# The low part of the down weights by an accumulating DMA from GpSimd

## Chip, cores and metric

The kernel runs on one core of a Trainium2 chip. The metric is the device time of one execution in microseconds; the table below has the median of three runs.

## What is computed

A decoder trunk of two layers over 512 tokens of width 1024: layer 0 mixes tokens by a gated delta rule, layer 1 by sliding-window attention, and both also attend to a memory. Each layer ends with a squared-ReLU MLP of hidden width 4096, and the down projection of that MLP is where the change lies:

```python
def sq_relu_mlp(h, w_up, w_down):
    return jnp.square(jax.nn.relu(h @ w_up)) @ w_down

...
        h = layer_norm(DN_ALPHA * h + sq_relu_mlp(h, mlp_w_up[layer], mlp_w_down[layer]),
                       ln_g[layer, 1], ln_b[layer, 1])
```

All of it is float32.

## The kernel before

TensorE multiplies in the format float32r, which keeps fewer bits than float32. So each operand is split into a high part (the value rounded to float32r) and a low part (the value minus the high part), and each product is made of three matmuls: high by high, high by low, low by high. For weights, `wload` (L81 to L89) makes the split: SyncE loads a slab of 128 x 1024 numbers (512 KB) into a buffer `wr`, ScalarE copies it into `wh` (L87, the rounding), and VectorE subtracts `wh` from `wr` into `wl` (L88). In the MLP the pool has four `wr` buffers and five each of `wh` and `wl`; each is used again as soon as its last reader is through.

`mlp` (L775 on) runs once per layer. The 4096 hidden features go in eight chunks c of 512. A chunk's down projection has two halves n of 512 output columns; each takes two slabs (`dn_slabs`, L947), and for each of four groups t of 128 tokens `down` (L936) makes 12 matmuls (`token_major`, L106 to L115: L112 reads `wh`, L113 `wl`, L114 `wh` with the low part of the hidden values) and VectorE adds the result to `res` (L945). Here one n of one c is called a half-chunk.

Between the down products stand the up products of the next chunk. They go by pairs of feature blocks in the class `Pair`: seven products m1 to m7 of 12 matmuls each (L866 to L868) into three PSUM tiles `upa`, `upb` and `upd`, on sums of weight blocks that GpSimd makes (`sa`, `sb`, L857 to L860) and that ScalarE and VectorE split at L118 and L119. In a steady half-chunk TensorE has m1, m6, m2, m5 and m7, then down for t = 0, m4, t = 1, m3, t = 2, t = 3. ScalarE copies the product m1 out of PSUM (L899) and VectorE adds it to `upb` (L905). The loop over c and n starts at L972; the first half-chunk of a layer has plain up products in place of a pair (`ups_second`, L816), and the last chunk (`downs_last`, L950) has no up products and takes four slabs at once.

The order on each engine is set by a scheduler that takes the program's order and the dependences; an engine works through its own list in order, and a wait holds up everything behind it. A buffer's next user waits for its last reader: a new `wh` for the L114 that read the old one, a new `wr` for the last reader of the old.

Of the kernel before, what the change touches and what calls it, by code (L numbers as in the profile page):

```python
# [11 lines left out]
F32 = mybir.dt.float32  # L12
F32R = mybir.dt.float32r
I32 = mybir.dt.int32
AF = mybir.ActivationFunctionType
ALU = mybir.AluOpType
AX = mybir.AxisListType

P = 128
# [30 lines left out]
def trunk(ctx: ExitStack, tc: tile.TileContext, xT, xn, memT, wk, wq, wv, wqm, wz, wmk, wmv, wo0, wo1, up, dn,  # L50
          bw, ws, conv, alog, dtb, nw, sinks, lng, lnb, lngb, pos, invf, out):
    nc = tc.nc
    V, G, A, T, SY = nc.vector, nc.gpsimd, nc.scalar, nc.tensor, nc.sync
# [8 lines left out]
    def nm(s):  # L62
        uid[0] += 1
        return f"{s}_{uid[0]}"
# [10 lines left out]
    def fr(ap):  # L75
        return ap.bitcast(F32)


    wpool = [None, 3, 4]

    def wload(src, shape):  # L81
        wp = wpool[0]
        raw = wp.tile(shape, F32, tag="wr", name=nm("wr"), bufs=wpool[1])
        SY.dma_start(raw, src)
        hi = wp.tile(shape, F32R, tag="wh", name=nm("wh"), bufs=wpool[2])
        lo = wp.tile(shape, F32R, tag="wl", name=nm("wl"), bufs=wpool[2])
        A.copy(hi, raw)  # L87
        V.tensor_sub(lo, raw, fr(hi))  # L88
        return hi, lo  # L89
# [685 lines left out]
    def mlp(pool, layer, last, gb0):  # L775
# [160 lines left out]
        def down(c, t, n, hid, slabs):  # L936
# [7 lines left out]
            else:  # L944
                V.tensor_tensor(dst, dst, ps, op=ALU.add)  # L945

        def dn_slabs(c, n):  # L947
            return [wload(dn[layer, c, n, i], [P, 2, 512]) for i in range(2)]

        def downs_last(hid):  # L950
            c = NC - 1
            slabs = [dn_slabs(c, n) for n in range(2)]
            late_out = []
            for t in range(NT):
                for n in range(2):
                    down(c, t, n, hid, slabs[n])
                    while late_out:
                        ln_out(*late_out.pop())
                if last:
                    mu, rs = ln_stats(t)  # L960
                    nmu = lns.tile([P, 1], F32, tag="nmu", name=nm("nmu"))
                    V.tensor_scalar(nmu, mu, -1.0, None, op0=ALU.mult)
                    late_out.append((t, nmu, rs, gb1))
                else:
                    ln_full(t, gb1)
            while late_out:
                ln_out(*late_out.pop())
# [4 lines left out]
        for c in range(NC - 1):  # L972
            later = new_hid()
            for n in range(2):
# [3 lines left out]
                if first:  # L978
                    ups_second(later)
                    slabs = dn_slabs(c, n)  # L980
                else:
                    p.m1()
                    p.m6()
                    p.split2()
                    slabs = dn_slabs(c, n)
                    p.m2()
                    p.m5()
                    p.m7()
# [26 lines left out]
    with tc.tile_pool(name="mlp0", bufs=2) as mpl:  # L1015
        mlp(mpl, 0, False, gb0)
# [185 lines left out]
    with tc.tile_pool(name="mlp1", bufs=2) as mpl:  # L1202
        mlp(mpl, 1, True, gb0)
# [71 lines left out]
```

## Time and profile before

| | |
|---|---|
| median of three runs (lowest to highest) | 1188.91 us (1188.09 to 1189.69) |
| the profiled execution's own time | 1191.65 us |
| its span, from the first to the last instruction | 1189.9 us |
| busy: TensorE, VectorE, ScalarE, GpSimd | 97%, 73%, 48%, 19% of the span |
| low parts by VectorE at L88 (all weights) | 136 in 166.4 us, 1225 ns each |
| copies to the high part at L87 | 136 in 142.5 us, 1051 ns each |
| loads of down weights | 64 of 512 KB, median 4.6 us from issue to landing |
| moved over the span | 114.17 MB, 96 GB/s |

In rows of a timeline the columns are the start in us from the span's start, the duration in us, the engine, the line, the operation, output and inputs, and in brackets how long the engine was idle before and for whom it waited. PE is TensorE (its matmuls overlap: the next starts before the row of one is over), DVE VectorE, ACT ScalarE, POOL GpSimd and SP SyncE; SPq is SyncE's queue.

### The profile page before, as it was taken

The page shows a single profiled execution, that of the slowest core. Times are in us where ns is not written, and L with a number is a line of the kernel's source. Part 1 is how long each engine was busy: PE and PEld are TensorE (multiplying, and loading weights), DVE is VectorE, ACT ScalarE, POOL GpSimd, SP SyncE. Part 2 cuts the span into 40 slices and gives each one's busy share as a digit, 9 for nine tenths or more (in the row PEclk, how much of TensorE's full clock was granted, in tenths as well). Part 3 has the DMA queues.
Part 4 walks back from the last instruction along what each step waited for, and adds up shares of the span by engine and source line. Part 5 has one row for each costly group of instructions (what it writes and reads, how often), then busy time and mean ns, then how long its engine had stood idle before and what let it go on. Part 6 is the DMA issues. An engine that isn't in the chain of part 4 may idle for free.

```text
span 1189.9 us, 19072 instructions
## 1 busy us (share of the span) xinstructions
PE 1158.1 (97%) x7512; PEld 1025.7 (86%) x7512; DVE 866.3 (73%) x1621; ACT 566.3 (48%) x1024; POOL 229.0 (19%) x180
## 2 busy tenths in 40 slices
PE   9899999999999999999999999999999999999996
PEld 8877788879998898998988888788989998989985
DVE  5478889777798666666656968886986666666657
ACT  5345454655484443545443346662653534445341
POOL 0112111101014413232220100000042314232204
PEclk9899999999999999999999999999999999999998
DMA  7522141204324232232424231112333242323311
GB/s 255 176 72 78 60 132 39 67 19 139 130 82 139 79 121 93 90 123 71 141 73 124 72 120 41 38 35 71 107 112 119 74 139 72 128 86 101 112 36 71
DMA packets 41242, 114.17 MB, mean 96 GB/s; under 512 B 12160, under 2 KB 12544, under 8 KB 41152
## 3 DMA queue, kind: packets, MB, share of 16 engines
q1 hardware_dynamic: 40576, 112.04, 28.9%
q8 instruction: 59, 0.97, 0.3%
q10 hardware_dynamic: 576, 0.92, 0.2%
q14 instruction: 31, 0.25, 0.1%
HBM read 109.53 MB, written 3.41 MB: 95 GB/s over the span
## 4 chain that ended last, share of the span: by engine, by line
PE 81%; DVE 11%; ACT 3%; DMA 1%; POOL 1%; issue 1%; POOLq 0%; SPq 0%; ACTq 0%; DVEq 0%
PE dn L113 9%; PE dn L114 9%; PE dn L112 9%; PE upb L866 3%; PE upb L867 3%; PE upb L868 3%; PE wo L113 2%; PE wo L114 2%; PE wo L112 2%; PE upa L867 2%; PE upd L867 2%; PE upa L868 2%; PE upd L868 2%; PE upa L866 2%; PE upd L866 2%; PE up L103 2%
## 5 line engine op out<-in xcount | busy, mean ns | idle before, releaser
L114 PE MATMUL dn<-wh,hl 128*128 128x512 f32 x512 | 200.0, 391 | 0.0
L113 PE MATMUL dn<-wl,hh 128*128 128x512 f32 x512 | 200.0, 391 | 0.0
L112 PE MATMUL dn<-wh,hh 128*128 128x512 f32 x512 | 199.6, 390 | 0.0
L87 ACT CAST wh<-wr 128x1024 fp32r<-128x1024 f32 (+1 forms) x136 | 142.5, 1051 | 103.8 <-PE dn L114 24.8
L88 DVE TENSOR_TENSOR wl<-wr,wh 128x1024 fp32r<-128x1024 f32 (+1 forms) x136 | 166.4, 1225 | 34.1 <-ACT wh L87 31.7
L114 PEld LDWEIGHTS dn<-wh,hl 128*128 128x128 f32 x512 | 96.1, 188 | 20.3
L945 DVE TENSOR_TENSOR res<-res,dn 128x512 f32<-128x512 f32 x120 | 82.0, 683 | 40.7 <-PE dn L114 40.2
L112 PEld LDWEIGHTS dn<-wh,hh 128*128 128x128 f32 x512 | 96.4, 188 | 17.6
L113 PEld LDWEIGHTS dn<-wl,hh 128*128 128x128 f32 x512 | 96.1, 188 | 17.7
L857 POOL TENSOR_TENSOR sa<-wr 128x512 f32<-128x512 f32 x26 | 36.1, 1388 | 370.6 <-DMA wr<-in_up_dram 279.6
L651 POOL TENSOR_TENSOR rs<-rs,nhalf 128x1 f32<-128x1 f32 x16 | 13.3, 834 | 338.1 <-DVE rs L650 282.0
L119 DVE TENSOR_TENSOR wl<-wr,wh 128x1024 fp32r<-128x1024 f32 x26 | 34.1, 1310 | 43.5 <-ACT wh L118 43.5
L118 ACT CAST wh<-sa 128x1024 fp32r<-128x1024 f32 x26 | 27.3, 1050 | 76.6 <-PE upd L867 76.6
L867 PE MATMUL upa<-XL,wh 128*128 128x256 f32 x208 | 58.5, 281 | 0.0
L867 PE MATMUL upd<-XL,wh 128*128 128x256 f32 x208 | 58.5, 281 | 0.0
L868 PE MATMUL upa<-XH,wl 128*128 128x256 f32 x208 | 58.4, 281 | 0.0
L868 PE MATMUL upd<-XH,wl 128*128 128x256 f32 x208 | 58.3, 280 | 0.0
L866 PE MATMUL upa<-XH,wh 128*128 128x256 f32 x208 | 58.3, 280 | 0.0
L866 PE MATMUL upd<-XH,wh 128*128 128x256 f32 x208 | 58.2, 280 | 0.0
L866 PE MATMUL upb<-TH,wh 128*128 128x256 f32 x208 | 58.0, 279 | 0.0
L867 PE MATMUL upb<-TL,wh 128*128 128x256 f32 x208 | 57.8, 278 | 0.0
L868 PE MATMUL upb<-TH,wl 128*128 128x256 f32 x208 | 57.6, 277 | 0.0
(411 smaller groups left out, 3365.7 us busy)
## 6 DMA issues: line engine op xcount, KB each, us to landing
wr<-in_up_dram SPq DMA_DIRECT2D x64, 512.0 KB, 5.4
wr<-in_dn_dram SPq DMA_DIRECT2D x64, 512.0 KB, 4.6
wr<-in_wo_dram SPq DMA_DIRECT2D x16, 512.0 KB, 3.8
wr<-in_bw_dram SPq DMA_DIRECT2D x8, 512.0 KB, 4.3
wr<-in_wz_dram SPq DMA_DIRECT2D x6, 520.0 KB, 4.5
wr<-in_wk_dram SPq DMA_DIRECT2D x6, 512.0 KB, 3.7
wr<-in_wq_dram SPq DMA_DIRECT2D x6, 512.0 KB, 3.5
wr<-in_wv_dram SPq DMA_DIRECT2D x6, 512.0 KB, 3.7
```

Source lines behind the costliest of these rows:

```text
L87: A.copy(hi, raw)
L88: V.tensor_sub(lo, raw, fr(hi))
L112: T.matmul(ps, sh, hi[:, kk, :], start=(k == 0), stop=False)
L113: T.matmul(ps, sh, lo[:, kk, :], start=False, stop=False)
L114: T.matmul(ps, sl, hi[:, kk, :], start=False, stop=(k == nk - 1))
L118: A.copy(hi, src)
L119: V.tensor_sub(lo, src, fr(hi))
L857: G.tensor_tensor(sa[:, 0], raw[1][:, kA], raw[1][:, kB], op=ALU.add)
L866: T.matmul(ps, hi[:, k, :], mh[:, k, :], start=start and k == 0, stop=False, skip_group_check=True)
L867: T.matmul(ps, hi[:, k, :], ml[:, k, :], start=False, stop=False, skip_group_check=True)
L868: T.matmul(ps, lo[:, k, :], mh[:, k, :], start=False, stop=stop and k == 3, skip_group_check=True)
L945: V.tensor_tensor(dst, dst, ps, op=ALU.add)
```

## The change

Only the down weights are loaded in a new way; all other weights keep `wload`. The raw slab is still loaded by SyncE and rounded by ScalarE. Then ScalarE writes the negated high part into `wl`, and a DMA issued from GpSimd reads the weights from memory once more and adds them onto it, so that `wl` holds the weights minus the high part.

```diff
+        def dn_load(src, shape):
+            wp = wpool[0]
+            raw = wp.tile(shape, F32, tag="wr", name=nm("wr"), bufs=wpool[1])
+            hi = wp.tile(shape, F32R, tag="wh", name=nm("wh"), bufs=wpool[2])
+            lo = wp.tile(shape, F32R, tag="wl", name=nm("wl"), bufs=wpool[2])
+            SY.dma_start(raw, src)
+            A.copy(hi, raw)
+            A.activation(lo, fr(hi), AF.Copy, scale=-1.0)
+            G.dma_start(lo, src, accum_op=ALU.add)
+            return hi, lo
+
         def dn_slabs(c, n):
-            return [wload(dn[layer, c, n, i], [P, 2, 512]) for i in range(2)]
+            return [dn_load(dn[layer, c, n, i], [P, 2, 512]) for i in range(2)]
```

The new function stands at L947 to L956, and lines behind it have numbers that are 11 higher. Where the instructions stand on ScalarE at the start of a steady half-chunk of layer 1, before (numbers in names tell buffers apart; `r` and `hh` are the hidden values of the pair before):

```order
L118 CAST hh_9417<-r_9477 128x1024
L87 CAST wh_9651<-wr_9649 128x1024
L87 CAST wh_9657<-wr_9655 128x1024
L899 COPY m_1465_9628<-upa_9615 128x256
L118 CAST wh_9740<-wr_9703 128x1024
L910 ACTIVATE r_9673<-upa_9615 128x256
```

and with the change:

```order
L118 CAST hh_9453<-r_9515 128x1024
L953 CAST wh_9688<-wr_9687 128x1024
L954 ACTIVATE wl_9689<-wh_9688 128x1024
L953 CAST wh_9695<-wr_9694 128x1024
L899 COPY m_1465_9666<-upa_9653 128x256
L954 ACTIVATE wl_9696<-wh_9695 128x1024
L118 CAST wh_9780<-wr_9743 128x1024
L910 ACTIVATE r_9713<-upa_9653 128x256
```

The first negation stands between the two copies, the second behind the copy of m1's product, `m`. On GpSimd there was before only the next pair's sums behind those of the last (in_dn_dram, below, is the weights in memory):

```order
L858 TENSOR_TENSOR sb_9512<-sa_9511,wr_9507 128x512
L860 TENSOR_TENSOR sb_9512<-wr_9507,sb_9512 128x512
L857 TENSOR_TENSOR sa_9707<-wr_9704 128x512
L859 TENSOR_TENSOR sa_9707<-wr_9703,wr_9704 128x512
L858 TENSOR_TENSOR sb_9708<-sa_9707,wr_9703 128x512
```

and with the change:

```order
L858 TENSOR_TENSOR sb_9550<-sa_9549,wr_9545 128x512
L860 TENSOR_TENSOR sb_9550<-wr_9545,sb_9550 128x512
L955 DMA wl_9689<-in_dn_dram 128x1024
L955 DMA wl_9696<-in_dn_dram 128x1024
L857 TENSOR_TENSOR sa_9747<-wr_9744 128x512
L859 TENSOR_TENSOR sa_9747<-wr_9743,wr_9744 128x512
```

Both DMAs stand ahead of the next pair's sums. The last place is ScalarE at the last chunk of layer 1, where four slabs are made; before:

```order
L87 CAST wh_11767<-wr_11765 128x1024
L87 CAST wh_11773<-wr_11771 128x1024
L932 ACTIVATE r_11643<-r_11643 128x768
L794 ACTIVATE r_11643<-r_11643 128x1024
L118 CAST hh_11387<-r_11643 128x1024
L87 CAST wh_11779<-wr_11777 128x1024
```

and with the change:

```order
L954 ACTIVATE wl_11828<-wh_11827 128x1024
L953 CAST wh_11834<-wr_11833 128x1024
L932 ACTIVATE r_11703<-r_11703 128x768
L954 ACTIVATE wl_11835<-wh_11834 128x1024
L794 ACTIVATE r_11703<-r_11703 128x1024
L118 CAST hh_11443<-r_11703 128x1024
L953 CAST wh_11841<-wr_11840 128x1024
L954 ACTIVATE wl_11842<-wh_11841 128x1024
```

The third slab's negation moved in between L932 and L794, ahead of the copy of the last hidden values and of the fourth slab.

## The prediction

> **What bounds the kernel now.** I read the page first: the span, the busy shares and the chain that ended last.
>
> ```profile
> span 1189.9 us, 19072 instructions
> PE 1158.1 (97%) x7512; PEld 1025.7 (86%) x7512; DVE 866.3 (73%) x1621; ACT 566.3 (48%) x1024; POOL 229.0 (19%) x180
> PE 81%; DVE 11%; ACT 3%; DMA 1%; POOL 1%; issue 1%; POOLq 0%; SPq 0%; ACTq 0%; DVEq 0%
> ```
>
> TensorE is busy for 97% of the span, and the chain is mostly its own matmuls. A share is an average, so next comes the view of the span in stages: a stretch of layer 1's MLP, the stretch between the MLPs, and the end.
>
> ```profile
> core 0: us, PE busy (x) PEld busy (x) DVE busy (x) ACT busy (x) POOL busy (x), PEclk, DMA share, GB/s
> 640.00:860.00 220.00, 215.10 (x1363) 183.11 (x1362) 181.56 (x471) 108.12 (x272) 7.52 (x8) 1.00 0.22 72
> 900.00:950.00 50.00, 50.00 (x311) 44.97 (x310) 33.75 (x39) 24.31 (x29) 18.25 (x12) 1.00 0.27 85
> 1140.00:1190.00 50.00, 39.55 (x203) 33.53 (x201) 33.32 (x52) 12.71 (x16) 12.66 (x12) 0.93 0.17 58
> ```
>
> In the MLP, where the change is, TensorE has no idle time (50.00 of 50.00), while VectorE works 33.75 of 50. So VectorE's work there is off the path, and the question is only whether the new way of making the low part is ready in time. For that I followed one half-chunk (the work of one n of one c) on TensorE and on the engines that feed it. TensorE's timeline:
>
> ```profile
> 928.46 0.39 PE L114 MATMUL dn<-wh,hl 128*128 128x512 f32 x1
> 928.68 0.28 PE L866 MATMUL upa<-XH,wh 128*128 128x256 f32 x1
> ...
> 935.92 0.40 PE L113 MATMUL dn<-wl,hh 128*128 128x512 f32 x1
> ...
> 937.29 0.39 PE L113 MATMUL dn<-wl,hh 128*128 128x512 f32 x1
> ```
>
> The old half-chunk's down products end at 928.68, five up products follow, and the new low parts are first read at 935.92 (slab 1) and, by the third of the product's four L113, at 937.29 (slab 2). ScalarE and VectorE make the slabs in between:
>
> ```profile
> 927.52 1.06 ACT L87 CAST wh<-wr 128x1024 fp32r<-128x1024 f32 x1 [0.24 <-PE dn L114]
> 928.88 1.05 ACT L87 CAST wh<-wr 128x1024 fp32r<-128x1024 f32 x1 [0.30 <-PE dn L114]
> 930.31 0.37 ACT L899 COPY m<-upa 128x256 f32<-128x256 f32 x1 [0.37 <-PE upa L868]
> 932.97 1.05 ACT L118 CAST wh<-wr 128x1024 fp32r<-128x1024 f32 x1 [2.29 <-PE upa L867]
> ...
> 928.61 1.23 DVE L88 TENSOR_TENSOR wl<-wr,wh 128x1024 fp32r<-128x1024 f32 x1
> 930.35 1.22 DVE L88 TENSOR_TENSOR wl<-wr,wh 128x1024 fp32r<-128x1024 f32 x1
> 931.75 0.42 DVE L905 TENSOR_TENSOR u<-m,upb 128x256 f32<-128x256 f32 x1 [0.18 <-PE upb L868]
> ```
>
> Both copies wait for TensorE to release a buffer, so a slab can't be prepared sooner than this. Before, the low parts are ready at 929.84 and 931.57, some 6.1 and 5.7 us before they are read. That slack is what the change spends.
>
> **The change part by part.** *Removed:* 64 subtractions on VectorE. By these rows that is 64 x 1.22 = 78 us, all in stages in which TensorE is never idle: worth nothing on the path. *Added on ScalarE:* 64 negations. I price them by the copy of the same tile, 1.05: 67 us beside 566, off the path except by what they delay. In the new order ScalarE runs copy 1, negation 1, copy 2, the copy of m, negation 2. Copy 1 ends at 928.58, negation 1 at 929.63, copy 2 at 930.68, m at 931.05 and negation 2 at 932.10. The next copy (932.97) isn't touched. The copy of m comes 0.37 later, so L905 ends at about 932.54. The product behind it that adds to upb is the last of the five, 7.0 / 5 = 1.4 us before 935.69, at 934.3: covered by 1.7 us, and past that each us would cost one.
>
> *Moved:* a wr buffer is free after the copy and not after the subtraction, so SyncE's loads start about 1.2 us earlier.
>
> ```profile
> 929.86 2.06 SPq L84 DMA_DIRECT2D wr<-in_dn_dram  x2
> 932.01 3.65 SPq L855 DMA_DIRECT2D wr<-in_up_dram  x2
> ```
>
> TensorE waits for none of these loads, so that is worth nothing; but they run from 928.6 on, just beside the new transfers.
>
> *Added on GpSimd:* 64 accumulating DMAs, each waiting for its negation, with TensorE waiting for them. Queued behind them on GpSimd are the four additions that make sa and sb; in this half-chunk they lie far from it:
>
> ```profile
> 924.18 1.31 POOL L860 TENSOR_TENSOR sb<-wr,sb 128x512 f32<-128x512 f32 x1
> ...
> 941.14 1.32 POOL L857 TENSOR_TENSOR sa<-wr 128x512 f32<-128x512 f32 x1 [15.65 <-DMA wr<-in_up_dram]
> ```
>
> GpSimd is idle from 925.5 to 941.1 and can issue at once. So transfer 1 has 935.92 - 929.63 = 6.3 us and transfer 2 937.29 - 932.10 = 5.2 us. Its latency L, from the issue to TensorE's release, is the disputed price; the trace shows no accumulating DMA and none from GpSimd. The nearest rows are plain loads of the same 512 KB:
>
> ```profile
> q1 hardware_dynamic: 40576, 112.04, 28.9%
> wr<-in_up_dram SPq DMA_DIRECT2D x64, 512.0 KB, 5.4
> wr<-in_dn_dram SPq DMA_DIRECT2D x64, 512.0 KB, 4.6
> L84 SPq DMA_DIRECT2D wr<-in_dn_dram x64: 327/328/384, 308.1 to 1139.7; - x64
> DMA to landing us min/median/max: 3.4/4.7/9.5
> ```
>
> The base is 4.6 us. An accumulation has to read two operands where a load reads one; a load's packets hold the 16 engines for 0.289 x 1189.9 x 0.524 / 112.04 = 1.6 us, so the second operand adds an estimated 1.6. GpSimd's share of issuing lies between SyncE's 0.33 and one of GpSimd's own additions, 1.3: I take 0.8. That makes 7.0. Transfer 2 is issued 2.5 us after transfer 1, whose packets then hold the engines for 3.2, so it finds 0.7 of them in its way: 7.7. Bounds: 3.4 (the fastest plain load, nothing added) to 9.5 + 1.6 + 1.3 + 0.7 = 13.1. I take 7.7, as the medians are from the same neighbourhood of other loads.
>
> The Trainium skill ("DMA: Bandwidth & Descriptors", "Anatomy of one DMA — SWDGE (gpsimd) path") gives 2.0 us + bytes / 436e3 for a DMA from GpSimd, an estimated 3.2 us for this size. By that rule the steady half-chunks cost nothing and the sum below is 2 x 0.7 = 1.4 us and not 74. The trace disagrees so far: no plain load of this size lands in under 3.4 us and the median is 4.6, so I stay with the rows.
>
> The sum. In a steady half-chunk transfer 1 is 0.7 late and transfer 2 is 7.7 - 5.2 = 2.5 us late; both stall the same stream, so the larger counts. There are 26 of them (13 in each layer): 26 x 2.5 = 65 us. The first half-chunk of a layer has room:
>
> ```profile
> 351.56 1.05 ACT L87 CAST wh<-wr 128x1024 fp32r<-128x1024 f32 x1 [0.47 <-PE up L103]
> 365.81 0.39 PE L113 MATMUL dn<-wl,hh 128*128 128x512 f32 x1
> ```
>
> With the negation the second slab is at 353.7, 12 us before its reading: nothing, and it would cost from L = 12 on. The last chunk makes four slabs, and the fourth is late:
>
> ```profile
> 1152.26 1.05 ACT L87 CAST wh<-wr 128x1024 fp32r<-128x1024 f32 x1 [7.30 <-PE upd L867]
> 1153.21 0.84 ACT L932 ACTIVATE r<-r 128x768 f32<-128x768 f32 x1
> 1154.08 1.06 ACT L794 ACTIVATE r<-r 128x1024 f32<-128x1024 f32 x1
> 1155.18 1.05 ACT L118 CAST hh<-r 128x1024 fp32r<-128x1024 f32 x1
> 1156.47 1.06 ACT L87 CAST wh<-wr 128x1024 fp32r<-128x1024 f32 x1 [0.24 <-PE dn L114]
> ...
> 1161.93 0.39 PE L113 MATMUL dn<-wl,hh 128*128 128x512 f32 x1
> ```
>
> The third negation now stands between L932 and L794, so the fourth copy ends at about 1158.4, its negation at 1159.4, and 2.5 us are left until 1161.93, the third L113 of that chunk's second product. With no transfer beside it L is 7.0: 4.5 us, twice, 9 us. Together 65 + 9 = 74 us. The profiled execution took 1191.65 (span 1189.9 and 1.75 around it) and would become 1265.7; it is 2.7 above the median of 1188.91, so the forecast for the median is **1263 us**.
>
> **The rivals.** *Hidden transfer.* If L stays at or below 5.2, the steady half-chunks cost nothing and only the last chunk pays, 2 x (L - 2.5): 1.8 us at 3.4 and 4.2 at 4.6, so 1190.7 to 1193.1. For it speaks that a plain load's median is below 5.2; against it, that the up loads already land at 5.4 and that nothing is then added for the second operand and the issue. This is also the case that the rule above of the Trainium skill leads to.
>
> *Much longer transfer.* If accumulation moves far slower than a load, or the two transfers and the loads at 929 to 935 delay each other, L goes to the upper bound of 13.1: 26 x 7.9 + 2 x (12.4 - 2.5) = 225 us, 1414. For it speaks the 9.5 us maximum of a plain load under others; against it, a DMA share of only 0.27 in the stage.
>
> *Faster, by relief of VectorE between the layers.* TensorE is idle for 4.9 us of 640 to 860. If the subtractions of layer 0's last slabs are what holds up VectorE there, their absence returns up to those 4.9 us: 1184. It decides only if L is below 5 as well, because otherwise the stalls outweigh it. Against it: VectorE has one such subtraction left in that stretch, 1.2 us.
>
> **How the numbers follow.** Forecast (L from 5.5 to 10) 0.52, much longer 0.23, hidden 0.20, relief 0.05. About 2.4 us, 0.2%, is what a measurement of this kernel can tell from no change. Hidden transfers are within that only at L below 3.7, so 0.08 of them counts as the same and 0.12 as slower: faster 0.05, same 0.08, slower 0.87. The range goes from 1192 (the relief and the shortest of the hidden transfers left out) to 1350, where transfer 2 has L = 10.8: 26 x 5.6 + 2 x 7.6 = 161 us, with the upper part of the much longer case left out.
>
> **What would show it.** Right: TensorE waits at L113 for a DMA, about 28 times, some 2.5 us each and some 4.5 in the two last chunks, and MLP stages in which it is no longer busy all the time; transfers that land in 7 to 8 us; ScalarE about 67 us busier and VectorE 78 us less. The forecast is wrong if the transfers land within 5 us and L113 waits for nothing, or if the wait is at another place: at upb for L905, at GpSimd's additions behind the DMAs, or at a load.

## The result, and the profile after

The changed kernel takes 1366.95 us (median of four executions, 1356.97 to 1377.81); the kernel before took 1188.70 beside it. The ratio is 1.146 (95% interval 1.1435 to 1.1491): slower, as forecast, but by 178 us where 74 were forecast, and outside the range. One execution of the changed kernel, in which the chip was in a slower state, is left out of the ratio. All rows below are from the execution of 1356.97, 165.3 us above the profiled one of before; two others took some 10 us more, at a mean granted clock of 0.94 where this one has 0.947.

The page of the changed kernel, in the order of the rows shown of before (span, busy shares, DMA queues, chain, and then the group of the low parts' matmuls and the loads):

```profile
span 1355.3 us, 19201 instructions
PE 1219.7 (90%) x7512; PEld 1056.5 (78%) x7512; DVE 829.1 (61%) x1557; ACT 622.6 (46%) x1088; POOL 273.8 (20%) x244
q1 hardware_dynamic: 40576, 112.04, 24.7%
q0 software_dynamic: 9216, 33.56, 14.1%
PE 54%; DMA 21%; DVE 9%; issue 9%; ACT 4%; POOL 2%; POOLq 0%; DVEq 0%; SPq 0%; ACTq 0%
L113 PE MATMUL dn<-wl,hh 128*128 128x512 f32 x512 | 221.2, 432 | 103.3 <-DMA wl<-in_dn_dram 103.3
wr<-in_dn_dram SPq DMA_DIRECT2D x64, 512.0 KB, 4.7
wl<-in_dn_dram POOLq DMA_DIRECT2D x64, 512.0 KB, 9.1
```

DMA had 1% of the chain that ended last and now has 21%. TensorE has the same 7512 matmuls, but they keep it busy for 1219.7 us instead of 1158.1. The new transfers land in 9.1 us while the plain loads still need 4.7. Their packets hold the 16 engines for 0.141 x 1355.3 x 0.524 / 33.56 = 2.98 us each, those of a load for 0.247 x 1355.3 x 0.524 / 112.04 = 1.57.

TensorE's waits, longest sum first:

```profile
PE dn L113 <- DMA wl<-in_dn_dram: 103.3, 55, 3.9
```

103.3 us of waiting and 61.6 us of longer matmuls (1219.7 - 1158.1) make 164.9 of the 165.3. The waits stand at the place that the prediction named; the longer matmuls stand around and behind them, and the prediction had none. ScalarE, GpSimd and SyncE in one steady half-chunk of layer 1:

```profile
1052.52 1.06 ACT L953 CAST wh<-wr 128x1024 fp32r<-128x1024 f32 x1 [0.24 <-PE dn L114]
1053.60 2.36 SPq L952 DMA_DIRECT2D wr<-in_dn_dram  x2
1053.60 1.06 ACT L954 ACTIVATE wl<-wh 128x1024 fp32r<-128x1024 f32 x1
1054.57 1.03 ACT L953 CAST wh<-wr 128x1024 fp32r<-128x1024 f32 x1
1054.96 0.88 POOL L955 DMA_DIRECT2D wl<-in_dn_dram  x1 [19.08 <-ACT wl L954]
1055.51 0.36 ACT L899 COPY m<-upa 128x256 f32<-128x256 f32 x1
1055.77 1.06 ACT L954 ACTIVATE wl<-wh 128x1024 fp32r<-128x1024 f32 x1
1057.12 0.86 POOL L955 DMA_DIRECT2D wl<-in_dn_dram  x1 [1.28 <-ACT wl L954]
1057.69 1.63 POOL L857 TENSOR_TENSOR sa<-wr 128x512 f32<-128x512 f32 x1
...
1060.58 3.77 SPq L855 DMA_DIRECT2D wr<-in_up_dram  x2
```

ScalarE runs in the order and at the pace of the working, and GpSimd issues as soon as a negation is done. But from 1053.6 on two loads of down weights are issued as well, and from 1060.6 on two of up weights. TensorE in the same half-chunk:

```profile
1053.68 0.28 PE L866 MATMUL upa<-XH,wh 128*128 128x256 f32 x1
...
1063.89 0.79 PE L113 MATMUL dn<-wl,hh 128*128 128x512 f32 x1 [2.82 <-DMA wl<-in_dn_dram]
1064.48 0.63 PE L114 MATMUL dn<-wh,hl 128*128 128x512 f32 x1
1064.91 0.63 PE L112 MATMUL dn<-wh,hh 128*128 128x512 f32 x1
...
1067.03 0.50 PE L113 MATMUL dn<-wl,hh 128*128 128x512 f32 x1 [0.21 <-DMA wl<-in_dn_dram]
1067.37 0.40 PE L114 MATMUL dn<-wh,hl 128*128 128x512 f32 x1
```

Transfer 1 is released 8.9 us after its issue (1054.96 to 1063.89), transfer 2 after 9.9 (1057.12 to 1067.03). Transfer 2 comes 13.35 us after the start of the half-chunk at 1053.68; the same reading stood at 8.61 before (937.29 - 928.68). Between the two, matmuls follow each other by 0.43 us instead of 0.23. The view by windows of 2 us shows why, in its column of the granted clock (PEclk, 1.00 is full speed), and how busy the 16 DMA engines are (their share can pass 1.00, as a packet counts whole where it starts):

```profile
core 0: us, PE busy (x) PEld busy (x) DVE busy (x) ACT busy (x) POOL busy (x), PEclk, DMA share, GB/s
1060.00:1062.00 2.00, 1.08 (x9) 0.76 (x7) 2.00 (x1) 0.00 (x0) 1.92 (x3) 1.00 1.01 246
1062.00:1064.00 2.00, 0.10 (x1) 0.11 (x1) 1.62 (x3) 0.00 (x0) 1.99 (x1) 0.89 1.07 217
1064.00:1066.00 2.00, 2.00 (x5) 1.61 (x6) 0.89 (x1) 1.05 (x1) 0.00 (x0) 0.50 0.90 340
1066.00:1068.00 2.00, 1.79 (x6) 0.93 (x6) 0.33 (x1) 0.00 (x0) 0.00 (x0) 0.76 0.49 199
1068.00:1070.00 2.00, 2.00 (x17) 1.87 (x16) 0.75 (x2) 0.19 (x1) 0.00 (x0) 1.00 0.02 6
```

The DMA engines are fully busy until the low parts are there and idle right after: it is a queue that is worked off. The granted clock falls to 0.50 near the end of the wait of 2.82 us and stays there for 0.44 + 2.00 + 0.96 = 3.4 us (a window's 0.89 means that 0.44 of its 2 us were at 0.50). The Trainium skill ("TensorE: Matmul & The Clock Gate", "Part 1: The HAM clock gate (the "warmup" mystery)") has it that the clock is halved after an idle window of about 3.4 us and comes back after as long a busy one. The rows agree on the 0.50 and on the 3.4 us, but not on the idle time: here the clock fell some 2.5 us into the idle stretch, which was over after 2.82.

In this half-chunk the low clock is over when transfer 2 is released. In others it is not; in the one that starts at 506.74 the release comes 12.78 us later, at 519.52, and the clock is still low in the window behind it:

```profile
518.00:520.00 2.00, 0.91 (x2) 0.48 (x2) 1.23 (x1) 0.15 (x1) 0.00 (x0) 0.50 0.95 375
520.00:522.00 2.00, 2.00 (x6) 1.52 (x6) 0.00 (x0) 0.00 (x0) 0.00 (x0) 0.50 0.06 23
```

Of the 26 steady half-chunks 22 have such a stretch at 0.50, nine of 3.4 us, twelve of 6.8 and one of 10.2. Four have none, though TensorE waited 1.9 to 2.8 us for transfer 1 in them.

**What the time went into.** The two steady stretches (from the first to the last start that TensorE's timelines show, 24 half-chunks) took 499.5 us before and 645.3 after, 6.07 more per half-chunk. Transfer 2 is released on average 13.52 us after the start (12.51 to 14.77), 4.91 late. The other 1.16 is the low clock that lasts beyond that release: nothing in half-chunks like the first one above, up to 2.8 us in others. The rest of the 61.6 us of longer matmuls costs nothing: those matmuls run between the two releases, where TensorE would otherwise wait for transfer 2.

### The profile page after: what moved, and what is told of

The parts are those of the page before. It is cut to its first block, busy times and chain, and to the rows that moved or that the text cites. A ratio compares the mean times of both kernels' runs of the same rounds, so it can differ in the third digit from the quotient of the medians.

```text
span 1355.3 us, 19201 instructions
## 1 busy us (share of the span) xinstructions
PE 1219.7 (90%) x7512; PEld 1056.5 (78%) x7512; DVE 829.1 (61%) x1557; ACT 622.6 (46%) x1088; POOL 273.8 (20%) x244
## 3 DMA queue, kind: packets, MB, share of 16 engines
q1 hardware_dynamic: 40576, 112.04, 24.7%
q0 software_dynamic: 9216, 33.56, 14.1%
## 4 chain that ended last, share of the span: by engine, by line
PE 54%; DMA 21%; DVE 9%; issue 9%; ACT 4%; POOL 2%; POOLq 0%; DVEq 0%; SPq 0%; ACTq 0%
DMA wl<-in_dn_dram 20%; PE dn L113 7%; PE dn L114 6%; PE dn L112 6%; PE wo L113 2%; PE wo L114 2%; PE wo L112 2%; PE up L103 2%; PE up L104 2%; PE up L102 2%; DVE y L315 1%; POOL wl L955 1%; PE upb L866 1%; PE upb L867 1%; PE upb L868 1%
## 5 line engine op out<-in xcount | busy, mean ns | idle before, releaser
L113 PE MATMUL dn<-wl,hh 128*128 128x512 f32 x512 | 221.2, 432 | 103.3 <-DMA wl<-in_dn_dram 103.3
L113 PEld LDWEIGHTS dn<-wl,hh 128*128 128x128 f32 x512 | 102.8, 201 | 148.2 <-DMA wl<-in_dn_dram 130.1
L114 PE MATMUL dn<-wh,hl 128*128 128x512 f32 x512 | 214.5, 419 | 0.0
L955 POOL DMA_DIRECT2D wl<-in_dn_dram x64 | 56.0, 875 | 575.0 <-ACT wl L954 508.6
L119 DVE TENSOR_TENSOR wl<-wr,wh 128x1024 fp32r<-128x1024 f32 x26 | 97.3, 3744 | 46.0 <-ACT wh L118 46.0
L88 DVE TENSOR_TENSOR wl<-wr,wh 128x1024 fp32r<-128x1024 f32 (+1 forms) x72 | 87.6, 1221 | 26.8 <-ACT wh L87 26.3
L87 ACT CAST wh<-wr 128x1024 fp32r<-128x1024 f32 (+1 forms) x72 | 75.2, 1050 | 57.4 <-PE kq L103 13.9
L953 ACT CAST wh<-wr 128x1024 fp32r<-128x1024 f32 x64 | 66.8, 1044 | 41.4 <-PE upd L867 24.3
L118 ACT CAST wh<-sb 128x1024 fp32r<-128x1024 f32 x26 | 27.2, 1047 | 113.6 <-POOL sb L860 113.6
L118 ACT CAST w2h<-wr 128x512 fp32r<-128x512 f32 x26 | 16.1, 620 | 132.2 <-PE upb L867 132.2
L954 ACT ACTIVATE wl<-wh 128x1024 fp32r<-128x1024 f32 x64 | 67.7, 1058 | 0.9
L651 POOL TENSOR_TENSOR rs<-rs,nhalf 128x1 f32<-128x1 f32 x16 | 12.2, 764 | 254.1 <-DVE rs L650 241.8
```

Of the source, the lines that this page charges most:

```text
L113: T.matmul(ps, sh, lo[:, kk, :], start=False, stop=False)
L114: T.matmul(ps, sl, hi[:, kk, :], start=False, stop=(k == nk - 1))
L118: A.copy(hi, src)
L119: V.tensor_sub(lo, src, fr(hi))
L955: G.dma_start(lo, src, accum_op=ALU.add)
```

## The experiments

The theory: the transfers are late because they share the DMA engines with four loads, and TensorE's clock falls behind the waits. The rivals: accumulation is slow in itself; the traffic harms something other than L113; the landing only follows TensorE's pace. Each kernel is the changed one with the edit shown. Times are medians, ratios are against the kernel before on the same chip.

**e1_fill: work in place of the wait.** Fourteen repeats of the first matmul of each t = 0 product stand ahead of it.

```diff
+            if t == 0:
+                for _ in range(14):
+                    T.matmul(ps, hh[:, 0, sl], slabs[0][0][:, 0, :], start=True, stop=True)
```

> TensorE repeats the first matmul of each half-chunk's first down product 14 times ahead of it (3.2 us of extra work a half-chunk, the result unchanged), so that it is busy while it would wait. If the wait itself lowers the granted clock: the wait at L113 shrinks from 103 us to under 30, the clock stays at 1.0 in the MLP, the matmuls behind it keep their 0.23 us pitch, and the time falls by 40 to 70 us, to about 1300. If the clock falls for another reason (the traffic, the power): the clock of the stage stays near 0.93 and the time is 1357 or more.

Measured: 1302.58 us, ratio 1.0945 (1.0921 to 1.0969), 64 us faster than the changed kernel with 448 matmuls more. The group of the matmuls that read the low parts (busy time, mean ns, wait), before and then in e1_fill:

```profile
L113 PE MATMUL dn<-wl,hh 128*128 128x512 f32 x512 | 200.0, 391 | 0.0
L113 PE MATMUL dn<-wl,hh 128*128 128x512 f32 x512 | 201.4, 393 | 6.3 <-DMA wl<-in_dn_dram 6.3
```

The mean is 393 ns here, 391 before and 432 in the changed kernel; the granted clock over the span is 0.995, and 0.947 in the changed kernel. 448 repeats at 0.228 us are 102; with the 6.3 and the span of before, 1189.9, this gives 1298.2, and the span is 1298.3. So without idling there is no loss to the clock. The 64 us are more than the low clock's 1.16 per half-chunk, because the low parts also came sooner: slab 2 could be read 12.2 to 13.4 us after the start in the six of 13 half-chunks of layer 0 that waited, and by 11.9 in the others. Why sooner, no run shows.

**e2_no_raw: no loads of raw down slabs.** The high part is copied from numbers that lie on the chip already, and the accumulation makes the low part to fit, so the products keep their work.

```diff
...
-            SY.dma_start(raw, src)
-            A.copy(hi, raw)
+            A.copy(hi, fr(XH[:, 0:2, :]))
...
```

> The raw down slabs are not loaded (the high part is copied from another tile, so the down products are of other numbers); the negations and the accumulating DMAs stay. If the 9.1 us of a transfer come from sharing the DMA engines with the loads: it lands in 5.5 to 7 us and the time is 1200 to 1270. If accumulation itself is that slow: it still lands in 8.5 us or more and the time stays within 30 us of 1357.

Measured: 1253.38 us, ratio 1.0527 (1.0494 to 1.0560).

```profile
wl<-in_dn_dram POOLq DMA_DIRECT2D x64, 512.0 KB, 5.8
```

The landing falls from 9.1 to 5.8, and transfer 2 is released 9.76 us after the start (mean of ten half-chunks of layer 0) instead of 13.25 in the same layer. The two loads left out held the engines for 2 x 1.57 = 3.1 us; the release came 3.5 sooner.

**e3_plain: a plain copy from GpSimd.** Without `accum_op` the DMA overwrites the negated part; the subtraction is left out.

```diff
-            G.dma_start(lo, src, accum_op=ALU.add)
+            G.dma_start(lo, src)
```

> The same DMA from GpSimd without the accumulation: it overwrites the negated part with the weights, so the low part is not the low part. If the second operand costs only engine time: the packets of a transfer hold the engines for about 1.6 us in place of 3.0, it lands in 6.5 to 7.5 us and the time is 1240 to 1290. If the add is slow in itself: it lands in 5 us or less, as a load from SyncE does, and the time is below 1210.

Measured: 1257.50 us, ratio 1.0576 (1.0514 to 1.0637). The transfers land in 7.3 us, hold the engines for 1.65 us each and are issued in 0.55 us instead of 0.87. So the second operand is worth 1.3 us of engine time and 1.8 of landing, and a DMA from GpSimd beside the four loads is late even without it: TensorE still waits 46.8 us for these transfers.

**e6_one_slab and e7_halves: less, and the same in pieces.** In the first only the second slab of a pair goes the new way; in the second each accumulation is cut into two of 256 KB.

```diff
-            return [dn_load(dn[layer, c, n, i], [P, 2, 512]) for i in range(2)]
+            return [f(dn[layer, c, n, i], [P, 2, 512]) for i, f in enumerate((wload, dn_load))]
```

```diff
-            G.dma_start(lo, src, accum_op=ALU.add)
+            for k in range(2):
+                G.dma_start(lo[:, k], src[:, k], accum_op=ALU.add)
```

> Slab 1 of each half-chunk is made as before (VectorE), slab 2 with the accumulating DMA, the result unchanged. By late transfers plus lower clock: one transfer a half-chunk, with some 5.9 us until it is read and about 7.5 us to land beside the loads, so 1.6 us of waiting and 1 us of lower clock in 26 half-chunks and a few us more in the last chunks: 1240 to 1290. If a transfer's latency is not made longer by the others: it stays at 9 us and the time is above 1300.

> Each slab's accumulation is issued as two DMAs of 256 KB, the result unchanged. If the sharing of the engines sets the landing: the first half is there earlier, the four together end as late as the two did, and the time falls by 10 to 40 us, to about 1330. If a fixed cost for each transfer and GpSimd's issue set it: the last lands 1 to 2 us later than before and the time is 1360 to 1420.

Measured: 1242.90 us, ratio 1.0436 (1.0388 to 1.0483), and 1360.36 us, ratio 1.1404 (1.1357 to 1.1452). One slab lands in 7.5 us and is released 10.19 after the start (mean of ten). Halves gain nothing, where the sharing of the engines had been expected to let them gain 10 to 40 us: the first half could be read sooner, but the last is released 14.3 to 15.0 us after the start in 23 of the 26 half-chunks, and each costs GpSimd 1.05 us to issue. GpSimd's last issue ends 5.1 us after the start instead of 4.3, and the engine time of a half-chunk is 12.8 us instead of 12.2.

**e4_unread, e8_short_sums and e9_late_read: nobody waits at t = 0.** In e4_unread the down products read `wh` in place of `wl`. e8_short_sums adds to this that GpSimd's sums are cut to an eighth and the splits of `sa` and `sb` read XH instead. In e9_late_read only t = 0 reads `wh`. Each leaves out what it doesn't read: the low part of the down weights, in e9 for t = 0 alone, and in e8 the sums too. The edit of e9_late_read:

```diff
-            token_major(ps, slabs, lambda k: hh[:, k, sl], lambda k: hl[:, k, sl])
+            use = [(h, h) for h, _ in slabs] if t == 0 else slabs
+            token_major(ps, use, lambda k: hh[:, k, sl], lambda k: hl[:, k, sl])
```

> All transfers run, but the down products read the high part in place of the low part, so nobody waits for them. If the waits and the clock behind them are the whole loss: 1188 to 1196, with a granted clock of 0.99. If the traffic, the negations or GpSimd's work slow something else as well: above 1210.

> As the kernel in which nobody reads the accumulated low part, and besides GpSimd's four sums are cut from 128x512 to 128x64 numbers each, with the two splits of the sums reading another tile in their place (the up products are then of other numbers). If VectorE's subtraction of the raw up slab, 3.7 us there in place of 1.2, is slow because GpSimd's sums run beside it: it is back at 1.2 to 1.4 us, TensorE no longer waits for VectorE at the last upb product, and the time is 1188 to 1200. If the transfers or their issue slow it: it stays above 3 us and the time above 1240.

> The changed kernel, except that the down product of t = 0 reads wh in place of wl; t = 1 to 3 read wl as before, so the low part is first read some 4 us later and all DMAs, buffers and splits stay (left out: the low part of the down weights in the first quarter of the tokens). It replaces the run in which nobody read wl and VectorE got the buffer of an unread low part. Theory (the time is lost in waiting at L113 and in the low clock behind it, the transfers' traffic itself costs nothing else): budgets of 10.3 and 9.2 us against a median landing of 9.1, so most waits are gone: 1190 to 1215 us, granted clock 0.99, VectorE no longer waiting for the transfers. Rival (the traffic of the new transfers slows other things as well: loads, GpSimd's sums, VectorE): still over 1235 us, with TensorE waiting at upb or upa.

Measured: 1263.40 us, ratio 1.0603 (1.0568 to 1.0638); 1259.70, ratio 1.0582 (1.0554 to 1.0611); 1220.79, ratio 1.0248 (1.0202 to 1.0294). The first two missed what was expected of the theory, by 67 and 60 us. A group of e4_unread shows that the edit had made a new wait:

```profile
L119 DVE TENSOR_TENSOR wl<-wr,wh 128x1024 fp32r<-128x1024 f32 x26 | 35.1, 1352 | 167.8 <-DMA wl<-in_dn_dram 159.9
```

A low buffer that nobody reads is free when its transfer lands, VectorE's next low part took just this buffer, and TensorE waited for VectorE (51.8 us at `upb`). Short sums didn't change that (162.1 us of the same wait). So these two runs say nothing on the traffic. e9_late_read keeps a reader for each buffer, and there the waits stand where t = 1 reads slab 2. Two of them, on TensorE's timeline:

```profile
500.66 0.50 PE L113 MATMUL dn<-wl,hh 128*128 128x512 f32 x1 [0.52 <-DMA wl<-in_dn_dram]
522.51 0.50 PE L113 MATMUL dn<-wl,hh 128*128 128x512 f32 x1 [0.60 <-DMA wl<-in_dn_dram]
```

Transfer 2 is released 13.1 to 14.8 us after the start wherever there is a wait (eleven of the 13 half-chunks of layer 0). The landing is as late with TensorE running on as with TensorE waiting. Given 4.2 us more, the kernel is 146 us faster than the changed one, the clock is 0.989, and 21.5 us of waits are left. TensorE's next longest wait, 2.7 us at another place, is in the kernel before too, so the traffic harms little else. The time is 6 us above the expected range because 4.2 us don't quite cover the 4.9.

**e5_from_sbuf and e12_loads_held: the engines for the accumulations alone.** e5_from_sbuf adds the raw slab on the chip instead of reading memory again; `wr` is then held until the landing, and so SyncE's next loads wait. e12_loads_held reads memory as before, but holds `wr` in the same way, by a DMA of 512 bytes that overwrites one column of it behind the landing.

```diff
-            G.dma_start(lo, src, accum_op=ALU.add)
+            G.dma_start(lo, raw, accum_op=ALU.add)
```

```diff
             G.dma_start(lo, src, accum_op=ALU.add)
+            SY.dma_start(raw[:, 0, 0:1], fr(lo)[:, 0, 0:1])
```

> The accumulating DMA reads the weights from the raw slab on the chip and not from memory again, the result unchanged. The raw buffer is then held until the transfer has landed, so the next loads start behind it and not beside it. If the loads beside it make the transfer late: it lands in 5.5 to 7 us and the time is 1220 to 1290. If the second operand and the add make it late: it lands in 8.5 us or more and the time is 1340 or more. If the loads that start later become the wait: TensorE's feeders wait for wr and the time is above 1360.

> The changed kernel, the accumulation from memory as it is, but each raw slab is held until its transfer has landed: a DMA of SyncE then writes one column of wl over the first column of wr, which nobody reads any more, so that the next load into this buffer, and the up loads behind it on SyncE, start after the landing. Nothing is left out; 64 DMAs of 512 bytes are added. In the changed kernel six transfers of 512 KB share the 16 DMA engines from the start of a half-chunk: two loads of down weights and two of up weights at 1.57 us of engine time each, and two accumulations at 2.98, 12.2 us in all, and transfer 2 is released 13.3 us after the start. Theory (the landing is set by this queue of engine time): the two accumulations have the engines for themselves, 6.0 us, and land in about 5.5 us, 9 to 10 us after the start, as in e5_from_sbuf: 1225 to 1250 us. Rival (e5 gained by its source on the chip, not by its later loads; reading memory for an accumulation is slow in itself): landing 7.5 us or more and 1280 us or more.

Measured: 1231.02 us, ratio 1.0348 (1.0321 to 1.0375), and 1269.31 us, ratio 1.0675 (1.0647 to 1.0703). The landings, of e5_from_sbuf and then of e12_loads_held:

```profile
wl<-wr POOLq DMA_DIRECT2D x64, 512.0 KB, 5.4
```

```profile
wl<-in_dn_dram POOLq DMA_DIRECT2D x64, 512.0 KB, 6.0
```

The timeline of e12_loads_held in its first steady half-chunk, which starts at 375.01:

```profile
376.74 0.89 POOL L955 DMA_DIRECT2D wl<-in_dn_dram  x1 [17.52 <-PE upa L868]
378.91 0.86 POOL L955 DMA_DIRECT2D wl<-in_dn_dram  x1 [1.28 <-ACT wl L954]
...
382.06 0.47 SPq L956 DMA_DIRECT2D wr<-wl  x1
382.70 0.48 SPq L952 DMA_DIRECT2D wr<-in_dn_dram  x1
...
385.08 0.50 PE L113 MATMUL dn<-wl,hh 128*128 128x512 f32 x1 [1.30 <-DMA wl<-in_dn_dram]
```

The loads start at 382.7, behind transfer 1, and transfer 2 is released 10.07 us after the start (11.0 on average, as the negations come later in the other half-chunks). The same DMA from the same memory lands in 6.0 us instead of 9.1 when the loads stand behind it: this is the separation that was wanted, and the rival "slow in itself" falls. The Trainium skill ("DMA: Bandwidth & Descriptors", "Issuing engines are not separate DMA queues") says that DMAs of all issuing engines run on the same 16 DMA engines and interleave; these rows agree. The expected time was missed by 19 us: held loads make the up weights and ScalarE late in turn. ScalarE waits 147.7 us for up weights, and TensorE waits for ScalarE's copy of m, which it never did in the changed kernel:

```profile
PE dn L113 <- DMA wl<-in_dn_dram: 36.6, 33, 2.6
PE upa L866 <- ACT m L899: 16.6, 18, 1.8
```

**e11_lo_last and e10_sbuf_lo_last: the low parts read last.** In the t = 0 product the four matmuls with `wl` come after the eight with `wh`; e11 on the changed kernel, e10 on e5_from_sbuf.

```diff
...
+                ks = [(s, kk, 2 * s + kk) for s in range(len(slabs)) for kk in range(2)]
+                for s, kk, k in ks:
+                    T.matmul(ps, hh[:, k, sl], slabs[s][0][:, kk, :], start=(k == 0), stop=False)
+                    T.matmul(ps, hl[:, k, sl], slabs[s][0][:, kk, :], start=False, stop=False)
+                for s, kk, k in ks:
+                    T.matmul(ps, hh[:, k, sl], slabs[s][1][:, kk, :], start=False, stop=(k == ks[-1][2]))
...
```

> The changed kernel with the order of e10_sbuf_lo_last alone: the four matmuls with wl last in the product of t = 0, the accumulation from memory as it is; nothing is left out. Theory: in a steady half-chunk transfer 1 is 2.8 us late and transfer 2 hardly at all behind it; transfer 1 gains 1.6 us, transfer 2 0.7, so each stall is 0.7 to 1.6 us shorter, 20 to 40 us in all, and the clock falls less behind shorter waits, another 20 to 40 us of the 62: 1290 to 1325 us. Rival (as for e10): 1350 or more.

> The accumulation takes the raw slab on the chip as its source (as in e5_from_sbuf), and in the product of t = 0 the four matmuls with wl come after the eight with wh; nothing is left out. The low part of slab 1 is read 7 matmuls later (1.6 us), that of slab 2 3 matmuls later (0.7 us). Theory: e5 waited some 0.7 us per half-chunk for transfer 2 and that wait goes: 1231 becomes 1203 to 1215, clock 0.99 to 1.00; what is left are the last chunk of a layer, where a transfer was 5.1 us late, and the copy of m behind the negations. It isn't faster than the kernel before. Rival (the landing moves with TensorE's own pace, so that a later reading is met by a later landing): 1225 or more.

Measured: 1366.52 us, ratio 1.1474 (1.1445 to 1.1503), and 1236.47 us, ratio 1.0369 (1.0336 to 1.0402). Both missed: nothing was gained. By their times alone both would speak for the rival, that the landing follows TensorE's pace; their traces show other reasons. In e11 the waits moved (TensorE, in the half-chunk that starts at 1002.60):

```profile
1012.86 0.73 PE L946 MATMUL dn<-wl,hh 128*128 128x512 f32 x2 [1.26 <-DMA wl<-in_dn_dram]
1015.99 1.22 PE L946 MATMUL dn<-wl,hh 128*128 128x512 f32 x2 [2.40 <-DMA wl<-in_dn_dram]
1017.01 0.41 PE L866 MATMUL upb<-TH,w2h 128*128 128x256 f32 x1
```

Transfer 2 is released 13.39 us after the start, just as in the changed kernel (13.35). The 1.6 us that slab 1 gained were never on the path, since slab 2 ends last; and the 0.7 that slab 2 gained went into the clock, as now no matmuls are left to run slowly ahead of the release: up products at 1017 still take 0.41 for 0.28. The expectation had taken the wait for transfer 1 for the loss. In e10 the waits at the low parts went down (23.2 us in e5_from_sbuf, 8.2 here), and another, of 4.7 us there, grew:

```profile
PE upa L866 <- ACT m L899: 15.4, 21, 1.8
PE dn L946 <- DMA wl<-wr: 8.2, 5, 4.9
```

The copy of m, behind copy 1, negation 1 and copy 2 on ScalarE, now keeps `upa` from the next product: a reader of that copy that the prediction had not priced, as it followed L905 and `upb` alone. In the changed kernel the copy ends 2.19 us after the start and nobody waits for it; here, where `wr` is held until the landing, it ends 3.39 after it on average.

None of these kernels is faster than the kernel before.

## Why the prediction was wrong

**Right.** The sign; the place (L113 waiting for the DMA); VectorE's and ScalarE's work off the path; ScalarE's order; the third L113 as the reading that decides; the issue by GpSimd (0.8 taken, 0.87 measured) and the second operand (1.6 taken; 2.98 - 1.57 = 1.4 of engine time, 1.8 of landing by e3_plain). The last chunks of the layers cost little: of the 165.3 us, 145.8 lie in the 24 half-chunks, the 13th of each layer adds some 12 in all, and some 7 are left, where 9 were forecast.

**Wrong: the term for other transfers.** The step that failed is "so it finds 0.7 of them in its way: 7.7", with its companion that the earlier loads are "worth nothing". L of transfer 2, from the end of its negation (3.15 us after the start) to its release (13.52), is 10.4 and not 7.7. "The same neighbourhood of other loads" did not hold: the trace of before had four loads per half-chunk, 4 x 1.57 = 6.3 us of engine time; now there are 6.3 + 2 x 2.98 = 12.2, issued in the first 10.7 us. With 12.2 us of work, the engines are done some 13 us after the start, and as the transfers interleave (in the half-chunk above, transfer 1 and a load issued 0.7 us behind it land within 0.2 us of each other), transfer 2 is done no sooner. Transfer 1, taken as 0.7 us late, is 3.0 late on average (10.22 after the start instead of 7.24), which is why TensorE waits 55 times and not 28. The sum was to hand in the rows of before: 1.6 for a load and 3.2 for an accumulation give 4 x 1.6 + 2 x 3.2 = 12.8. The DMA share of 0.27, quoted against the longer transfer, was a mean over a stage whose load comes in one burst; in the trace of before, in a half-chunk that starts at 501.34, the share (the column before the last) is 0.73 to 0.87 and then 0.10:

```profile
503.00:505.00 2.00, 2.00 (x20) 2.00 (x19) 1.65 (x3) 0.34 (x1) 0.00 (x0) 1.00 0.73 215
...
507.00:509.00 2.00, 2.00 (x17) 1.91 (x16) 1.36 (x2) 0.52 (x1) 0.00 (x0) 1.00 0.87 332
...
511.00:513.00 2.00, 2.00 (x17) 1.87 (x16) 0.97 (x2) 0.00 (x0) 0.00 (x0) 1.00 0.10 35
```

So the term of the steady half-chunks was 26 x 4.9 = 128 us and not 65.

**Wrong: a term that was missing.** The sum took a wait to cost its own length. In 22 of the 26 half-chunks the granted clock fell to 0.50 at waits of 2.1 to 3.5 us, which cost 1.16 us per half-chunk beyond the release, 26 x 1.16 = 30 us. Either error alone would have left the time inside the range: 128 and 9 alone give some 1326 us, 65, 9 and 30 some 1293. All three terms, 128, 30 and the measured 7, make the 165 us of the profiled execution; the 10 us by which the median lies higher have no trace.

**The rivals.** The much longer transfer was the right one in mechanism: "the two transfers and the loads ... delay each other" is what e2_no_raw and e12_loads_held show. The rule of 3.2 us by the Trainium skill ("DMA: Bandwidth & Descriptors", "Anatomy of one DMA — SWDGE (gpsimd) path"), from which the hidden transfer followed, is far from every run: 9.1 beside four loads, 7.3 there without the accumulation, 5.8 beside two, 5.4 to 6.0 with the loads held back. No run here has a plain DMA from GpSimd with nothing beside it. The relief of VectorE between the layers was outweighed by the stalls, and no run isolates it.

## What to carry to other kernels

Price a new transfer by the queue that it joins: add up the engine time of every DMA issued in the same stretch, and take the last landing from that sum, not from the median of the transfers seen without it. Here e2_no_raw has 9.2 us of engine time in a half-chunk and the release 9.76 after the start, e6_one_slab 9.3 and 10.19, the changed kernel 12.2 and 13.52; e1_fill is the exception, with 12.0 and in half of its half-chunks a release by 11.8. Then ask what an earlier release elsewhere (here of the raw buffer) puts in front of it. And a recurring wait of some 3 us on TensorE is to be priced above its length, by the half clock that outlasts it (in this case 1.16 us on average); of matmuls that run slowly ahead of a later wait, nothing is to be added.

## What was not expected of the hardware

VectorE's subtraction `wl<-wr,wh` took 1310 ns on average before and 3744 in the changed kernel, where GpSimd's sums run at the same time:

```profile
L119 DVE TENSOR_TENSOR wl<-wr,wh 128x1024 fp32r<-128x1024 f32 x26 | 97.3, 3744 | 46.0 <-ACT wh L118 46.0
```

With short sums (e8_short_sums) it took 1240 ns, and in e4_unread, where it started later, 1352. This fits a path to the on-chip memory that the two engines share, as the Trainium skill ("GPSIMD Engine Reference", "1. Specifications") states for instructions with two inputs there; no run changed the overlap alone, and here it was off the path.
